# A two-layer gMLP and MLA encoder on one core: the order of its large stages from a list of jobs with due times, with 116 seven-product pairs, activations kept in DRAM and taps by VectorE

## The chip, the cores and the metric

The kernel runs on one core of a Trainium2 chip. The metric is device time in microseconds (us), the median of several runs. Profiles come from one profiled execution. Engines: PE is TensorE, PEld its weight loads, DVE is VectorE, ACT is ScalarE, POOL is GpSimd, SP issues most DMAs.

## What is computed

The input x has 256 tokens of width 2048, in float32. There are two layers. Each has a token mixer and a convolutional feed-forward part; behind each comes `x <- LayerNorm(ALPHA * x + sublayer(x))`.

```python
# layer 0, mixer (gMLP); u and v have 6144 columns, 8 groups, windows of 128 tokens
u, v = split(gelu(x @ w_in), 2);  v = layer_norm(v)
s = einsum('gij,bnjgd->bnigd', w_s * mask, v) + b_s
m = (u * s) @ w_out
# layer 1, mixer (latent attention): 16 heads, ranks 512, chunk-causal softmax, then @ w_out
# both layers, feed-forward (D_FF = 5504)
h = causal_depthwise_conv3(x @ w_up) + conv_b;  a, g = split(h, 2)
f = (silu(g) * a) @ w_down
```

## The kernel before

**Products.** Every float32 operand is split into a high part (float32r) and the low rest; a product is then three matmuls (high × high, high × low, low × high). Activations are kept transposed, as the stationary operand; weights stream as 512 columns. The weights come from DRAM as a list of steps of 128 × 2048 (`Step`, L50), one 1 MiB load each on SP's queue. ScalarE casts a step's high part (`wh`), VectorE subtracts for the low part (`wl`). In the stages v, u and up and in wo and dn a step holds a pair of k-tiles against 1024 output columns, so a plain pair is 2 k-tiles × 2 token blocks × 2 column halves × 3 products, 24 matmuls (`Square.plain`, L469).

**Seven-product pairs.** For some pairs the two k-tiles, two token blocks and two column halves are taken as 2 × 2 blocks and multiplied with seven products instead of eight, Strassen's way (`Square.step`, L477): 21 matmuls. VectorE then also forms sums of weight quarters (four adds of 512 columns, in place in `raw`), ScalarE casts them (`th`), VectorE takes their low part (`tl`); the low part `wl` covers 1536 columns (`Feed._split`, L141). The activations need sums too: `sums_quad` (L432) once for a stage, `sums1` (L438) per pair in wo and dn. Four further PSUM banks (`_p`) collect products and `Square.gather` (L505) adds them together after the last seven-product pair. Which pairs are such is fixed in L236 to L240, where `placed` also says at which of a square's eight steps they stand: v three in five squares of six, u two in six, up two in nine of ten per layer, wo five in each half, dn four in each half.

**Stages.** v and u: six squares of eight steps each (x against 6144 columns each). Behind each v square ScalarE applies gelu and VectorE takes statistics; the six v tiles stay in SBUF until u's gates use them. Behind each u square the `gates` (L862) transpose u, multiply v by the window weights (PE), and form the gated values (VectorE). wo and dn (`Down`, L569 on) run over their k-tiles in two halves of 1024 columns, forward and then backward; `split4` (L397) makes the high and low part of the gate values or activations for each half. up: four steps for the first 512 columns (`boundary`, L653), ten squares of eight steps and two last steps. Behind each up square PE transposes the result into four PSUM banks (`ht`), and `taps` (L928) apply the convolution to four tiles of 128 × 256 at a time: ScalarE makes three scaled copies of each tile, VectorE adds them in two adds of 1020 and 1016 columns per four tiles, ScalarE applies silu, VectorE multiplies. Then come the attention stages (L1049 on), where `scores` (L1252) makes, for each head and token block, five matmuls of 256 columns.

**Order of the work.** Instructions run in program order on each engine. `Feed.next` (L198) is called before each PE step: it splits up to two steps ahead and loads about two more, as far as the 22 slots of 8 KiB a partition (`BIG`) allow. Side work (taps, gates, gathers, statistics) is put at a number of steps from now and at one of three places within a step (`Flow`, L86). All instructions go through one recording line, so rows of the profile show L74; tiles tell them apart.

## Time and profile before

| | us |
|---|---|
| median of 3 runs | 2484.49 (2484.10 to 2484.86) |
| profiled execution | 2485.57 |
| its span, first to last instruction | 2483.8 |
| VectorE, ScalarE busy | 2049.6, 1444.2 |

In the profile a row of a group gives engine, operation, tiles written and read, shape and count, then busy time and the mean duration in ns, then the idle time before it and what ended that. A row of a window gives start and end, its length, then busy time and (xcount) of PE, PEld, DVE, ACT and POOL, the granted PE clock, the DMA share and GB/s. In a timeline the first two numbers are start and duration in us. Durations overlap at their ends: a 512-column matmul shows 0.39 us, and the next one starts 0.23 us after it.

### The profile page before, as it was taken

To read this page: it belongs to the slowest core of one execution; us is meant where nothing else is said; L and a number is where in the kernel's file an instruction comes from. 1 tells how busy PE (TensorE), PEld (TensorE's weight loads), DVE (VectorE), ACT (ScalarE), POOL (GpSimd) and SP (SyncE) were. 2 spreads that over 40 slices of the span, in tenths; PEclk is the share of its full clock that TensorE was granted. 3 is DMA by queue.
4 is the path that set the end of the run, shared out by engine and by line. 5 is a ranking of instruction groups with operands and counts; after the bars stand their busy time and mean duration, and the time that the engine had idled before them with its cause. 6 is when DMAs were issued, how large, how long until landed. Compare 5 with 4: busy or idle time off the path is not lost.

```text
span 2483.8 us, 30045 instructions
## 1 busy us (share of the span) xinstructions
PE 2470.1 (99%) x11666; PEld 2068.6 (83%) x11666; DVE 2049.6 (83%) x2121; ACT 1444.2 (58%) x1673; POOL 1.9 (0%) x11
## 2 busy tenths in 40 slices
PE   9999999999999999999999999999999999999998
PEld 7888888888888888888888888988888888888886
DVE  7899888889797678888899887757768888889796
ACT  6455645555454566666665454555466666667552
POOL 0000000000000000000000000000000000000000
PEclk9999999999999999999999999999999999999999
DMA  7555645555666645555456665435555555556664
GB/s 308 191 193 197 206 167 170 202 171 203 220 214 235 229 166 174 204 186 203 153 198 237 226 237 210 173 136 213 203 174 207 171 187 202 189 196 202 226 205 151
DMA packets 119662, 492.64 MB, mean 198 GB/s; under 512 B 13280, under 2 KB 13664, under 8 KB 104928
## 3 DMA queue, kind: packets, MB, share of 16 engines
q1 hardware_dynamic: 118512, 484.31, 55.6%
q10 hardware_dynamic: 1008, 6.42, 0.6%
q8 instruction: 91, 1.49, 0.2%
q14 instruction: 51, 0.42, 0.0%
HBM read 482.29 MB, written 8.39 MB: 198 GB/s over the span
## 4 chain that ended last, share of the span: by engine, by line
PE 98%; DVE 1%; DMA 0%; ACT 0%; issue 0%; DVEq 0%; ACTq 0%
PE up L74 30%; PE dn L74 16%; PE u L74 9%; PE wo L74 9%; PE v L74 9%; PE up_p L74 4%; PE mo L74 4%; PE upf L74 2%; PE dn_p L74 2%; PE v_p L74 2%; PE ht L74 1%; PE u_p L74 1%; PE wo_p L74 1%; PE mkv L74 1%; PE kn L74 1%; PE qn L74 1%
## 5 line engine op out<-in xcount | busy, mean ns | idle before, releaser
L74 DVE TENSOR_TENSOR wl<-raw,wh 128x2048 fp32r<-128x2048 f32 (+3 forms) x456 | 955.5, 2110 | 216.6 <-ACT wh L74 202.9
L74 ACT CAST wh<-raw 128x2048 fp32r<-128x2048 f32 (+3 forms) x456 | 804.3, 1784 | 187.9 <-DMA raw<-in_ffn_up_dram 54.4
L74 PE MATMUL up<-wh,xhl 128*128 128x512 f32 x2056 | 563.8, 390 | 0.0
L74 PEld LDWEIGHTS up<-wh,xhl 128*128 128x128 f32 x2056 | 384.4, 188 | 78.8
L74 ACT CAST th<-raw 128x1024 fp32r<-128x1024 f32 x178 | 188.5, 1088 | 414.2 <-DVE raw L74 342.1
L74 PE MATMUL up<-wl,xhl 128*128 128x512 f32 x1028 | 319.6, 389 | 0.0
L74 DVE TENSOR_TENSOR raw<-raw 128x512 f32<-128x512 f32 x356 | 246.4, 692 | 12.3
L74 DVE TENSOR_TENSOR tl<-raw,th 128x1024 fp32r<-128x1024 f32 x178 | 214.8, 1222 | 20.7 <-ACT th L74 19.6
L74 PEld LDWEIGHTS up<-wl,xhl 128*128 128x128 f32 x1028 | 192.9, 188 | 40.3
L74 ACT ACTIVATE c<-ht,cst 128x256 f32<-128x256 f32 x320 | 160.0, 591 | 83.2 <-PE ht L74 83.2
L74 PE MATMUL wo<-wh,woa 128*128 128x512 f32 x628 | 173.2, 389 | 0.0
L74 PE MATMUL u<-wh,xhl 128*128 128x512 f32 x600 | 166.1, 391 | 0.0
L74 PE MATMUL dn<-wh,dn0a 128*128 128x512 f32 x576 | 158.3, 389 | 0.0
L74 PE MATMUL dn<-wh,dn1a 128*128 128x512 f32 x576 | 158.0, 389 | 0.0
L74 PE MATMUL v<-wh,xhl 128*128 128x512 f32 x558 | 155.2, 393 | 1.6 <-ACT wh L74 1.6
L74 PEld LDWEIGHTS wo<-wh,woa 128*128 128x128 f32 x628 | 117.7, 188 | 24.3
L74 PEld LDWEIGHTS u<-wh,xhl 128*128 128x128 f32 x600 | 111.9, 188 | 22.7
L74 PEld LDWEIGHTS dn<-wh,dn1a 128*128 128x128 f32 x576 | 108.0, 188 | 22.5
L74 PEld LDWEIGHTS dn<-wh,dn0a 128*128 128x128 f32 x576 | 108.0, 188 | 22.4
L74 PEld LDWEIGHTS v<-wh,xhl 128*128 128x128 f32 x558 | 105.6, 189 | 25.2 <-ACT wh L74 2.8
L74 PE MATMUL wo<-wl,woa 128*128 128x512 f32 x314 | 99.5, 389 | 0.0
L74 PE MATMUL u<-wl,xhl 128*128 128x512 f32 x300 | 93.4, 389 | 0.0
(510 smaller groups left out, 3577.7 us busy)
## 6 DMA issues: line engine op xcount, KB each, us to landing
raw<-in_ffn_up_dram SPq DMA_DIRECT2D x320, 512.0 KB, 4.8
raw<-in_ffn_dn_dram SPq DMA_DIRECT2D x172, 512.0 KB, 4.7
raw<-in_gm_in_dram SPq DMA_DIRECT2D x99, 512.0 KB, 4.9
raw<-in_gm_wout_dram SPq DMA_DIRECT2D x96, 512.0 KB, 4.4
raw<-in_gm_in_dram SPq DMA_DIRECT2D x46, 1024.0 KB, 4.9
raw<-in_ml_out_dram SPq DMA_DIRECT2D x16, 1024.0 KB, 4.8
raw<-in_ml_b_dram SPq DMA_DIRECT2D x14, 1024.0 KB, 4.9
raw<-in_ffn_up_dram SPq DMA_DIRECT2D x12, 1024.0 KB, 6.3
```

The costliest lines, as they stand in the source:

```text
L74: r = f(*args, **kw)
```

## The change

- **Planner.** In v, u, wo, up and dn, `Flow` and the look-ahead of `Feed.next` are replaced by `Plan`: every load, cast, subtraction, sum, gather, output pass, gate and tap is a `Job` with an engine, an estimated cost, predecessors, a due time and the slots (`big`, `bank`, `mid`, `t2`) that it needs and frees. `Plan.run` simulates the engines' clocks and, each time, emits the job whose due time plus three times the idle time that it would cause is least. Transposes (`turn`) are emitted between PE steps when their inputs are reckoned ready, and without fail before a square's first seven-product step. The other stages keep `Flow`.
- **Pairs.** u gets three seven-product pairs per square, four of the ten up squares three and the other six two (the first square included), wo seven and six, dn six and five: 116 for 89.
- **Weight sums.** Of the four 512-column adds two become one of 1024 columns; the gather's last two adds become one.
- **DRAM.** Five of the six v tiles go to DRAM (`park`, on SP's queue) and come back before u's gates. Five of the six wo sources (gate values) and five of the six tiles of feed-forward activations of a layer go to DRAM and come back once for each half. Residual, LayerNorm-row and table loads now keep program order on SP's queue.
- **Taps.** ScalarE makes one scaled copy (tap 2 and bias); the other two taps are multiply-adds by VectorE of 255 and 254 columns that read the transposes' PSUM banks, two for each tile.
- **Scores.** The first token block multiplies only its 128 keys.

The diff, cut to its core:

```diff
-            b21, x, y, b12 = (raw[:, i * 512 : (i + 1) * 512] for i in range(4))
-            b22, b11 = (x, y) if s.by_k else (y, x)
-            first, second = self._pairs(s)
-            ve.tensor_tensor(b11, b11, b12, ALU.subtract)
-            ve.tensor_tensor(b12, b22, b12, ALU.subtract)
-            ac.copy(first(s.th), first(raw))
-            ve.tensor_tensor(b22, b22, b11, ALU.add)
-            ve.tensor_tensor(b21, b21, b22, ALU.subtract)
-            ac.copy(second(s.th), second(raw))
+            q = self._quarters
+            c0, c1, c2, c3 = (raw[:, i * 512 : (i + 1) * 512] for i in range(4))
+            two = raw[:, 512:1536].rearrange("p (a c) -> p a c", a=2)
+            last = c3.rearrange("p (a c) -> p a c", a=1).to_broadcast([P, 2, 512])
+            ve.tensor_tensor(q(raw, 1), two, last, ALU.subtract)
+            ac.copy(q(s.th, 1), q(raw, 1))
+            ve.tensor_tensor(c2, c2, c1, ALU.add)
+            ve.tensor_tensor(c0, c0, c2, ALU.subtract)
+            ac.copy(q(s.th, 0), q(raw, 0))
...
+FIRST_BANKS = (0.0, 0.2, 2.7, 2.9)
+SUM_BANKS = (1.3, 2.0, 2.7, 3.4)
...
+def adds(n, k=1):
+    return k * (0.065 + 0.00106 * n)
+
+
+def copies(n, k=1):
+    return k * (0.07 + 0.00086 * n)
+
+
+def maps(n, k=1):
+    return k * (0.19 + 0.0009 * n)
...
+class Plan:
+    LAG = {"V": 0.16, "A": 0.33, "P": 0.21, "S": 1.9}
+    AHEAD = 60.0
...
+    def _prepare(self, j, load=None):
+        f = self.feed
+        s = f.steps[j]
+        cols = 1536 if s.seven else s.cols
+        after = (load,) if load else ()
+        c = self.chain[j]
+        new = lambda eng, cost, fn, after, kind, **kw: c.append(self.job(eng, cost, fn, after, step=j, kind=kind, **kw)) or c[-1]
+        hi = new("A", copies(cols), lambda: f.cast(j), after, "hi", need={"big": 2})
+        if not s.seven:
+            new("V", adds(cols), lambda: f.low(j), (hi,), "lo", give={"big": 1})
+            return
+        lo = new("V", adds(cols), lambda: f.low(j), (hi,), "lo")
+        one = new("V", adds(1024), lambda: f.sum1(j), (lo,), "t1")
+        th1 = new("A", copies(1024), lambda: f.high(j, 1), (one,), "h1", need={"big": 2})
+        two = new("V", adds(512, 2), lambda: f.sum2(j), (one,), "t2")
+        th2 = new("A", copies(1024), lambda: f.high(j, 0), (two, th1), "h2")
+        l1 = new("V", adds(1024), lambda: f.rest(j, 1), (th1,), "l1")
+        new("V", adds(1024), lambda: f.rest(j, 0), (th2, l1), "l2", give={"big": 1})
+
+    def _more(self):
+        f = self.feed
+        while self.made < min(f.used + 9, len(f.steps), self.last):
+            j = self.made
+            load = self.job("S", 2.9, f._load, self.loads[-1:], step=j, kind="load", need={"big": 1})
+            self.loads.append(load)
+            self.chain[j] = [load]
+            self._prepare(j, load)
+            self.made += 1
+
+    BEFORE = dict(load=12.0, hi=2.9, lo=0.2, t1=4.3, h1=2.7, t2=3.0, h2=1.5, l1=1.4, l2=0.2)
+    SEVEN = dict(hi=7.6, lo=5.6, load=12.0)
...
+            best = {}
+            for j in self.jobs:
+                if any(a.end is None for a in j.after) or not self._fits(j):
+                    continue
+                t = self._start(j)
+                idle = max(t - self.now[j.eng], 0.0)
+                key = (self._due(j) + 3.0 * idle, t)
+                if t > until and must() :
+                    continue
+                if j.eng not in best or key < best[j.eng][0]:
+                    best[j.eng] = key, t, j
...
+    def step(self, fn, after=(), banks=(), force=False):
+
+        f = self.feed
+        i = f.used
+        s = f.steps[i]
+        self.spare = 0
+        self.run(must_true, self.now["P"] - 0.3)
+        if force:
+            self.turnings(True)
+        else:
+            self.turnings()
+        self.spare = len(banks)
+        self._more()
+        must = lambda: (all(j.end is not None for j in self.chain[i]) and len(self.room["bank"]) >= len(banks)
+                        and all(j.end is not None for j in after))
+        self.run(must, self.now["P"])
+        t = max([self.now["P"]] + [j.end for j in self.chain[i]] + [j.end for j in after])
+        for i_, wait in enumerate(banks):
+            t = max(t, self.room["bank"][i_] - wait)
+        del self.room["bank"][: len(banks)]
+        self.spare = 0
+        self.run(must_true, t)
+        f.used += 1
+        fn(s)
+        self.now["P"] = t + s.len
+        del self.chain[i]
+        self.free("big", f.size(i), self.now["P"] + self.LAG["P"])
+        return self.now["P"] + self.LAG["P"]
+
+    def park(self, src, dst, after):
+
+        return self.job("S", 2.9, lambda: self.feed.sq.dma_start(dst, src()), after, due=0.0, give={"big": 1})
+
+    def fetch(self, src, tile, after, due):
+        return self.job("S", 2.9, lambda: self.feed.sq.dma_start(tile, src), after, due=due - 6.0, need={"big": 1})
...
-GROUP_U = [placed((2, 3), (4, 6))] * 6
-GROUP_UP = [placed((), ())] + [placed((2, 3), (4, 6))] * 9
-SEVEN_WO = ((8, 16, 24, 32, 40), (14, 20, 26, 32, 38))
-SEVEN_DN = ((8, 16, 24, 32), (12, 18, 26, 34))
+GROUP_U = [placed((2, 3, 4), (3, 5, 6))] * 6
+GROUP_UP = [placed((2, 3), (5, 6)), placed((2, 3), (4, 6)), placed((2, 3, 4), (4, 5, 6)), placed((2, 3), (4, 6)), placed((2, 3, 4), (4, 5, 6)), placed((2, 3), (4, 6)), placed((2, 3, 4), (4, 5, 6)), placed((2, 3), (4, 6)), placed((2, 3, 4), (4, 5, 6)), placed((2, 3), (4, 6))]
+SEVEN_WO = ((8, 14, 20, 26, 30, 34, 40), (40, 34, 28, 22, 16, 12))
+SEVEN_DN = ((8, 14, 18, 22, 26, 32), (34, 28, 22, 16, 12))
...
-        def gather(self, name):
-
-            e = slot([P, 4, 512], name)
-            u2 = tp.tile([P, 512], F32, tag="t2", name=f"{self.tag}u2", bufs=T2)
+        def gather(self, name, t, due):
+
+            e = self.e = slot([P, 4, 512], name)
             p1, p5, p6, p7 = self.p
-            ac.copy(e[:, 0], p1)
-            ve.tensor_tensor(u2, e[:, 0], p6, ALU.add)
-            ve.tensor_tensor(e[:, 2], u2, p7, ALU.add)
-            ve.tensor_tensor(e[:, 1], u2, p5, ALU.add)
-            ve.tensor_tensor(e[:, 3], e[:, 2], p5, ALU.add)
-            self.e, self.p = e, None
-
-        def out(self, name, func=None):
+
+            def add():
+                ve.tensor_tensor(e[:, 1], e[:, 0], p6, ALU.add)
+                ve.tensor_tensor(e[:, 2], e[:, 1], p7, ALU.add)
+                odd = e.rearrange("p (a b) c -> p a b c", b=2)[:, :, 1]
+                ve.tensor_tensor(odd, e[:, 1:3], p5.rearrange("p (a c) -> p a c", a=1).to_broadcast([P, 2, 512]), ALU.add)
+
+            one = plan.job("A", copies(512), lambda: ac.copy(e[:, 0], p1), ready=t, due=due, need={"big": 1})
+            self.gathered = plan.job("V", adds(512, 2) + adds(1024), add, (one,), due=due + 2, give={"bank": 4})
...
+        if gi < 5:
+            v_out.append(outside(f"vout{gi}"))
+            v_out[gi] = v_out[gi], plan.park(lambda vt=vt: flat(vt), v_out[gi], stat_jobs[-2:])
...
+    def v_back(gi, t):
+
+        after = (root,)
+        if gi < 5:
+            v[gi] = slot([P, 4, 512], f"vb{gi}")
+            after += (plan.fetch(v_out[gi][0], flat(v[gi]), (v_out[gi][1],), t),)
+        scaled[gi] = plan.job("A", maps(1024, 2), lambda: v_scale(gi), after, ready=t - 20, due=t)
...
-            c = slot([P, 2, 4, S], f"c{name}")
-            d = tp.tile([P, 4, S], F32, tag="mid", name=f"d{name}", bufs=MID)
-
-            def scale():
-                for i, (F, src) in enumerate(tiles):
-                    w = C_CONV + (layer * 2 * NF_FF + F) * 4
-                    ac.activation(c[:, 0, i], src, AF.Identity, bias=cst[:, w + 3 : w + 4], scale=cst[:, w + 2 : w + 3])
-                    ac.activation(c[:, 1, i], src, AF.Copy, scale=cst[:, w + 1 : w + 2])
-                    ac.activation(d[:, i], src, AF.Copy, scale=cst[:, w : w + 1])
-
-            y = c[:, 0, 0:n]
+            y = tp.tile([P, 4, S], F32, tag="mid", name=f"y{name}", bufs=MID)
+            w = lambda F, i: cst[:, C_CONV + (layer * 2 * NF_FF + F) * 4 + i :][:, 0:1]
+
+            def scale(i):
+                F, src = tiles[i]
+                ac.activation(y[:, i], src, AF.Identity, bias=w(F, 3), scale=w(F, 2))
+
+            def add(i):
+                F, src = tiles[i]
+                for d in (1, 2):
+                    ve.scalar_tensor_tensor(y[:, i, d:S], src[:, 0 : S - d], w(F, 2 - d), y[:, i, d:S], ALU.mult, ALU.add)
...
+        def tapped(tiles, name, t, bank, after=(), more=0):
+
+            a, m = tiles[0][0], len(tiles) // 2
+            scale, add, silu, gate = taps(tiles, name)
             made = []
-            flow.at(t, "mid", lambda: (made.extend(taps(tiles, f"{layer}_{a}")), made[0]()))
-            for i in range(1, 4):
-                flow.at(t + 1 + i, "mid", lambda i=i: made[i]())
+            for i in range(2 * m):
+                due = plan.wide - 0.4 - 0.7 * (2 * m - 1 - i + 4 * more) if bank else t + 6 + i
+                j = plan.job("A", maps(256), lambda i=i: scale(i), after if i == 0 else (j,), ready=t, due=due - 1.2,
+                             need={} if i else {"mid": 1})
+                made.append(plan.job("V", adds(255, 2), lambda i=i: add(i), (j, *made[-1:]), ready=t, due=due,
+                                     give={} if i < 2 * m - 1 else {"bank": 2} if bank else {"t2": 2}))
+            j = made[-1:]
+            j = (plan.job("A", maps(256 * m), silu, j, due=t + 18, need={"t2": 1}),)
+
+            def gated():
+                gate()
+                for F in range(a, a + m):
+                    gate_jobs[F].end = last.end
+
+            last = plan.job("V", adds(256 * m), gated, (*j, *order[0]), due=t + 20, need={"big": 1} if a % 8 == 0 else {},
+                            give={"t2": 1, "mid": 1})
+            order[0] = (last,)
+            if a % 8 == 6:
+                i = a // 8
+                dn.give(i, lambda: flat8(act[i]), (last,), lambda: slot([P, 4, 2 * S], f"ab{layer}_{i}"),
+                        lambda t: t.rearrange("p a (b c) -> p a b c", b=2))
...
-            o = sc[:, b * S : (b + 1) * S]
-            mm(o, q[:, 0, c], k[:, 0], b == 0, False)
-            mm(o, q[:, 0, c], k[:, 1], False, False)
-            mm(o, q[:, 1, c], k[:, 0], False, False)
-            mm(o, r[:, c], krh, False, False)
-            mm(o, r[:, c], krl, False, b == 1)
+            n = (b + 1) * P
+            o = sc[:, b * S : b * S + n]
+            mm(o, q[:, 0, c], k[:, 0, 0:n], b == 0, False)
+            mm(o, q[:, 0, c], k[:, 1, 0:n], False, False)
+            mm(o, q[:, 1, c], k[:, 0, 0:n], False, False)
+            mm(o, r[:, c], krh[:, 0:n], False, False)
+            mm(o, r[:, c], krl[:, 0:n], False, b == 1)
```

More of the change, by code (lines that the diff above doesn't have):

```diff
@@ new lines, in sum1, with sum2 @@
+    def sum1(self, j):
+        raw = self.raw[j]
+        two = raw[:, 512:1536].rearrange("p (a c) -> p a c", a=2)
+        last = raw[:, 1536:2048].rearrange("p (a c) -> p a c", a=1).to_broadcast([P, 2, 512])
+        self.ve.tensor_tensor(self._quarters(raw, 1), two, last, ALU.subtract)
+    def sum2(self, j):
+        c0, c1, c2 = (self.raw[j][:, i * 512 : (i + 1) * 512] for i in range(3))
+        self.ve.tensor_tensor(c2, c2, c1, ALU.add)
+        self.ve.tensor_tensor(c0, c0, c2, ALU.subtract)
@@ L555, in tock, with square @@
         flow.t += 1
-    def square(tag, order, xs, sums, name, room):
+    def square(tag, order, xs, sums, name, keep):
         sq = Square(tag)
         sevens = [i for i, (_, sv) in enumerate(order) if sv]
+        plan.wide = plan.at(feed.used + (sevens[0] if sevens else 8)) + 1.3
         for i in range(len(order)):
-            s = tick(room(i))
-            sq.step(s, xs, sums, i == len(order) - 1)
+            plan.keep = keep[i]
+            k0 = order[i][0] * 2
+            first = sevens and i == sevens[0]
+            after = (sums[k0][1],) if order[i][1] else ()
+            sq.t = plan.step(lambda s: sq.step(s, xs, {k: r for k, (r, _) in sums.items()}, i == len(order) - 1),
+                             after, FIRST_BANKS if i == 0 else SUM_BANKS if first else (), bool(first))
@@ L564, in square, with __init__ @@
             if sevens and i == sevens[-1]:
-                flow.at(1, "first", lambda: sq.gather(name))
-            tock()
+                sq.gather(name, sq.t, sq.t + 3)
         return sq
     class Down:
-        def __init__(self, n_k, src8, sevens, tag):
-            self.n_k, self.src8, self.sevens, self.tag = n_k, src8, sevens, tag
+        def __init__(self, n_k, gates, sevens, tag):
+            self.n_k, self.gates, self.sevens, self.tag = n_k, gates, sevens, tag
             self.hl, self.sums = {}, {}
-        def need(self, k, half):
+            self.quads = range((n_k + 3) // 4)
+            kept = {k // 4 for k in back_order(n_k, 0)[-KEEP:]}
+            self.left = {}
+            for half in range(2):
+                for i in [q // 2 for q in self.quads if half == 0 or q not in kept] + [k // 8 for k in sevens[half]]:
+                    self.left[half, i] = self.left.get((half, i), 0) + 1
+            self.last = (n_k - 1) // 8
+            self.parked, self.here = {}, {}
@@ new lines, in give, with source @@
+        def give(self, i, tile, after, again, view, stays=None):
+            if stays is not None:
+                self.here[0, i] = self.here[1, i] = stays, ()
+                return
+            dst = outside(f"{self.tag}src{i}")
+            self.parked[i] = dst, plan.park(tile, dst, after), again, view
+        def source(self, i, half, due):
+            if (half, i) not in self.here:
+                dst, job, again, view = self.parked[i]
+                t = again()
+                self.here[half, i] = view(t), (plan.fetch(dst, flat(t), (job,), due),)
+            return self.here[half, i]
@@ L576, in need, with done, f @@
+        def done(self, i, half):
+            def f(t):
+                self.left[half, i] -= 1
+                if self.left[half, i] == 0 and (half == 1 or i != self.last):
+                    plan.free("big", 1, t)
+            return f
+        def need(self, k, half, due):
             q = k // 4
             if q not in self.hl:
-                self.hl[q] = split4(self.src8[k // 8], q, min(4, self.n_k - 4 * q), f"{self.tag}a{half}_{q}")
-        def need_sums(self, k, half):
+                n = min(4, self.n_k - 4 * q)
+                src, after = self.source(k // 8, half, due - 6)
+                self.hl[q] = split4(src, q, n, f"{self.tag}a{half}_{q}",
+                                    {*after, *(self.gates[4 * q + i] for i in range(n))}, due, self.done(q // 2, half))
@@ L609, in run @@
                         if left == 5:
-                            ln.prep()
+                            plan.job("S", 6.0, ln.prep, due=plan.at(feed.used), need={"big": 2})
+                        plan.keep = 3 if 5 < left < 8 else 1
                     if half == 1 and left < LATE:
-                        late.append((s, {k // 4: hl[k // 4]}, left == 0))
-                        tock()
+                        late.append((plan.hold(), {k // 4: hl[k // 4][0]}, left == 0))
                         continue
-                    sq.step(s, hl, sums, left == 0)
+                    first = k in sevens and fresh
@@ L616, in run @@
+                    fresh = fresh and not first
+                    after = [hl[k // 4][1]] + ([sums[k][1]] if k in sevens else [])
+                    t = plan.step(lambda s: sq.step(s, {q: h for q, (h, _) in hl.items()},
+                                                    {q: r for q, (r, _) in sums.items()}, left == 0),
+                                  after, FIRST_BANKS if i == 0 else SUM_BANKS if first else (), first)
                     rest = order[i + 1 :]
```

477 lines of the change are left out of this document (358 added, 119 removed).

## Prediction

> **What bounds the kernel now.** I read the page's shares and its chain of waits first, then who TensorE (PE) waited for, then stretches of steady work in each stage.
>
> ```profile
> span 2483.8 us, 30045 instructions
> PE 2470.1 (99%) x11666; PEld 2068.6 (83%) x11666; DVE 2049.6 (83%) x2121; ACT 1444.2 (58%) x1673; POOL 1.9 (0%) x11
> PE 98%; DVE 1%; DMA 0%; ACT 0%; issue 0%; DVEq 0%; ACTq 0%
> ```
> ```profile
> PE v L74 <- ACT wh L74: 1.6, 1, 1.6
> PE warm L74 <- POOL idle L324: 1.3, 1, 1.3
> ```
>
> The chain that ends last is PE for 98%, and in the whole run PE waited twice, 2.9 us together, at the start. A busy PE alone need not be PE at its rate, so I look at how its matmuls follow one another, and at the other engines by stage (columns: PE, weight load, DVE, ACT, POOL, clock, DMA share, GB/s):
>
> ```profile
> 1305.34 18.36 PE dn L74 x81
> ```
> ```profile
> 0.00:50.00 50.00, 47.01 (x187) 35.85 (x188) 33.42 (x32) 29.23 (x28) 1.90 (x11) 0.97 0.84 332
> 89.29:213.73 124.44, 124.44 (x550) 103.04 (x550) 116.71 (x114) 67.97 (x58) 0.00 (x0) 1.00 0.53 189
> 297.37:487.50 190.13, 190.13 (x937) 160.56 (x937) 158.08 (x176) 102.28 (x109) 0.00 (x0) 1.00 0.51 173
> 557.38:660.00 102.62, 102.62 (x454) 84.94 (x454) 88.49 (x89) 57.16 (x44) 0.00 (x0) 1.00 0.61 220
> 908.95:1216.48 307.53, 307.53 (x1416) 256.29 (x1415) 264.02 (x239) 203.45 (x274) 0.00 (x0) 1.00 0.54 188
> 1260.00:1369.00 109.00, 109.00 (x505) 91.02 (x504) 96.32 (x96) 71.77 (x81) 0.00 (x0) 1.00 0.61 218
> 1369.00:1480.00 111.00, 111.00 (x492) 91.90 (x491) 92.35 (x94) 59.38 (x47) 0.00 (x0) 1.00 0.64 230
> 2473.20:2483.80 10.60, 0.00 (x0) 0.00 (x0) 7.50 (x13) 0.29 (x1) 0.00 (x0) 0.62 0.33 126
> ```
>
> 81 matmuls of 512 columns in 18.36 us are 226.7 ns each, back to back at clock 1.00. PE has no gap in any stage; 10.6 us behind its last matmul are the last LayerNorm and its store, which the change leaves alone. So the time is the count of matmuls times their rate: fewer matmuls shorten the run one for one, unless another engine then fails to feed PE. VectorE (DVE) is the candidate: it is at 94% in v (116.71 of 124.44), 83% in u, 86% in wo's first part, 86% in the up stage and 87% in dn.
>
> **PE's part of the change.** A plain pair of k-tiles takes 24 matmuls (2 k-tiles, 2 token blocks, 2 column halves, 3 products), a seven-product pair 21. Before: v 15, u 12, up 18 per layer, wo 10, dn 8 per layer, 89 in all. After: v 15, u 18, up 24, wo 13, dn 11, 116 in all. 27 × 3 = 81 matmuls go, 18.4 us by the row above. The number of sums that a square gathers costs PE nothing.
>
> The attention scores of the first token block shrink from 256 columns to 128 (16 heads × 5 = 80 matmuls). The trace has the old form, 128-column transposes, and 128-column float32 products:
>
> ```profile
> 1661.49 0.49 PE L74 MATMUL pt<-ident,p 128*128 128x128 f32 x3
> 1661.81 0.82 PE L74 MATMUL o<-pts,vv 128*128 128x256 f32 x4
> ...
> 1663.16 0.52 PE L74 MATMUL sc<-kn,qn 128*128 128x256 f32 x3
> 1663.52 0.40 PE L74 MATMUL sc<-krr,qr 128*128 128x256 f32 x2
> 1663.76 0.52 PE L74 MATMUL sc<-kn,qn 128*128 128x256 f32 x3
> 1664.11 0.40 PE L74 MATMUL sc<-krr,qr 128*128 128x256 f32 x2
> 1664.35 0.63 PE L74 MATMUL mo<-wh,oT 128*128 128x512 f32 x2
> ```
> ```profile
> 356.41 0.39 PE L74 MATMUL s<-wT,v 128*128 128x128 f32 x2
> 356.63 0.27 PE L74 MATMUL uT<-ident,u 128*128 128x128 f32 x1
> ```
>
> Ten score matmuls take 1.19 us, 0.119 each; three transposes of 128 columns take 0.32, 0.107 each, hardly less, as if the weight load of 128 columns set the pace. So I take 80 × 0.012 = 1.0 us off. Ends: by the line through 512 and 256 columns (0.227, 0.119) 128 columns would take 0.065, 4.3 us off; if the short product took float32's path (a pair of s instructions, 0.22), 8.1 us on. The transposes are the nearest row. The Trainium skill (TensorE: Matmul & The Clock Gate, "Back-to-back issue gap") gives about 81 ns for a sustained 128-column stream; by that the estimate would be 3.0 us off in place of 1.0. The transposes at 0.107 speak against it.
>
> Sum for PE: 18.4 + 1.0 = 19.4 us off. The profiled execution took 2485.6 (span 2483.8 and 1.8 around it), 1.1 above the median of the runs; so 2466.2 in its terms, 2465.1 in the median's, if nothing waits.
>
> **What it loads on VectorE.** Rows of seven steady up squares (14 seven-product pairs), one of u and one tile of wo:
>
> ```profile
> L74 DVE TENSOR_TENSOR wl<-raw,wh 128x2048 fp32r<-128x2048 f32 x43 | 97.7, 2287 | 1.2 <-ACT wh L74 1.2
> L74 DVE TENSOR_TENSOR raw<-raw 128x512 f32<-128x512 f32 x56 | 38.8, 692 | 2.0
> L74 DVE TENSOR_TENSOR tl<-raw,th 128x1024 fp32r<-128x1024 f32 x28 | 33.5, 1222 | 7.2 <-ACT th L74 7.2
> L74 DVE TENSOR_TENSOR wl<-raw,wh 128x1536 fp32r<-128x1536 f32 x14 | 24.6, 1755 | 32.4 <-ACT wh L74 32.4
> L74 DVE TENSOR_TENSOR c<-c,d 128x1016 f32<-128x1016 f32 x14 | 17.0, 1218 | 0.5
> L74 DVE TENSOR_TENSOR c<-c 128x1020 f32<-128x1020 f32 x14 | 17.0, 1215 | 0.0
> ```
> ```profile
> L74 DVE SCALAR_TENSOR_TENSOR sg<-s,cst,sb 128x256 f32<-128x256 f32 x32 | 13.9, 478 | 17.5 <-PE s L74 17.5
> ```
> ```profile
> L74 DVE TENSOR_TENSOR wos_14t<-v,wos_14t x1: 293/293/293, 736.0 to 736.0; 128x128 f32<-128x128 f32 x1
> L74 DVE TENSOR_TENSOR wos<-wos_14t,wos x1: 686/686/686, 740.7 to 740.7; 128x512 fp32r<-128x512 f32 x1
> ```
>
> - A pair made seven: low part 1.76, sums 1.22 (two quarters at once, priced as the 1024-wide row) + 2 × 0.69, tl 2 × 1.22, less the plain low part 2.29: +4.5 us. A pair that was seven saves 0.17 (one 1024-wide sum for two of 512), a gather 0.15 likewise.
> - Taps: the two adds of four tiles go, 34.0/7 = 4.9 us per square; 16 multiply-adds of 255 columns out of PSUM come, nearest row sg, 13.9/32 = 0.43 apart (0.48 alone): 7.0 (7.7). +2.1 us (+2.8). ScalarE loses two of three tap passes, so it is no bound.
> - A wo or dn pair also needs its activation sums: 4 × 0.29 + 0.69 = 1.85.
>
> u: 158.08/4 = 39.5 per square of 47.5; +4.5 − 0.5 gives 43.5 in 46.9 (93%). wo: 86% to about 92%. dn: 188.7 of 220, +3 × (4.5 + 1.85) − 1.7 gives 206 of 218 (95%). up: 264.02/7 = 37.7 of 43.9; with two sevens 39.3, with three (four of ten squares) 43.8 against PE's 43.25: over by 0.6. The kinds alternate, so two squares want 83.1 of 87.2 (95%). Below 100% everywhere once neighbours share; v ran at 94% with no wait of PE. What hides the new work is thus VectorE's idle time, plus the split steps ahead of PE. If that cover fails in the eight overfull squares alone, 8 × 0.6 = 5 us come on; I take 2 us, nearer to v's none.
>
> **DMA and its queue.** Gate values and activations leave in 20 transfers of 1 MiB (5 v, 5 wo sources, 5 per dn) and come back in 35: 58 MB on top of
>
> ```profile
> DMA packets 119662, 492.64 MB, mean 198 GB/s; under 512 B 13280, under 2 KB 13664, under 8 KB 104928
> ...
> raw<-in_ffn_up_dram SPq DMA_DIRECT2D x320, 512.0 KB, 4.8
> ...
> parked<-res ACTq DMA_DIRECT2D x6, 1024.0 KB, 6.1
> res<-parked SPq DMA_DIRECT2D x6, 1024.0 KB, 7.4
> ```
>
> wo gets most: ten fetches in some 225 us add 47 GB/s to 220; the first 50 us carried 332. So bandwidth is no bound. The new thing is order: SP's queue is serial, and a store that waits for VectorE's or ScalarE's last gate now holds every weight load queued behind it. A load that slips by one PE step (24 × 0.227 = 5.4 us) still lands (4.8) within that step, and the freed SBUF slots let loads run further ahead; zero, and 20 × 0.6 = 12 us if each store held a load two steps and the landing 0.6 us were all uncovered. I keep zero as value. The residual, LayerNorm-row and table loads now keep their place in the same queue; all are due some steps ahead of use: zero.
>
> **Forecast.** 2465.1 + 2 = 2467 us. Unknown sizes alone reach from 2461 (scores −4.3 in place of −1.0, no waits) to 2476 (scores +8.1).
>
> **Rivals.**
> (B) VectorE's idle share cannot go under the 6.2% of v. Then a pair of up squares takes 83.1/0.938 = 88.6 in place of 87.2, 1.4 × 8 = 11 us; dn 206/0.938 = 219.6 in place of 218, 1.6 × 2 = 3; u at 93% just fits. 2465.1 + 14 = 2479, and less if it binds in part. For: v is the fullest stage shown. Against: v's idle time there was no need, PE never waited.
> (C) Half of today's idle time stays because it is latency between engines:
>
> ```profile
> DVE wl L74 <- ACT wh L74: 33.6, 9, 4.9
> ```
>
> In those seven squares VectorE idled 43.5 us, mostly on that line. With half, 3.1 per square: 83.1 + 6.2 − 87.2 = 2.1 × 8 = 17 us in up, and u 43.5 + 4.0 − 46.9 = 0.6 × 6 = 4: 2486, no change. Against: the list puts other work into such waits. The Trainium skill (Perfetto Trace Analysis, "Identifying the Most-Contended Engine") judges TensorE by its weight loads, 83% here, level with VectorE, and so would take an edit that loads VectorE for a poor trade; PE's two short waits show that as yet VectorE limits nothing.
> (D) Slower. The planner prices a tap multiply-add at 0.335 us (its formula for 255 columns) where the sg row has 0.43: it believes the 16 taps of a square done 1.6 us before they are. Until then they hold the four PSUM banks that the square's first seven-product step needs, and PE's next matmul stands behind that wait. If VectorE has no slack left there, 1.6 × 20 squares = 32 us: 2497. It decides from 19.4/20 = 1.0 us per square on. Against: the taps are due before that step, four plain steps (21.8 us) lie ahead of it, and VectorE has in that time 7.0 us of taps and six 512-wide adds and gates (4.1 us at 0.69).
> That the change did not remove what it says would show as 11666 matmuls again; the lists of pairs leave no room for it.
>
> **How the numbers follow.** Forecast with its sizes (2461 to 2471): 0.60. B, whole or in part (2471 to 2479.5): 0.15. C (2479.5 to 2489.5): 0.09. D and other stalls beyond: 0.16. Runs of this kernel lie 0.8 us apart; 0.2%, 5 us, is about what a measurement can tell. Faster 0.75, same 0.09, slower 0.16. Range 2461 to 2485: it leaves out D above, about half of C, and little below.
>
> **What would show it.** Right: 11585 matmuls; PE idle under 20 us in all; VectorE near 95% in up and dn; ScalarE's busy time down; scores' first five matmuls about 0.107 apart; DMA near 550 MB. Wrong: PE waiting on wl or tl in up squares with three sevens (B, C), or on an ht bank that VectorE's taps still read at the first seven-product step (D), or weight casts waiting on raw loads behind a store.

## The result, and the profile after

The changed kernel takes 2467.11 us (median of 4 runs, 2466.72 to 2467.49), the kernel before 2484.40 beside it: 17.3 us less, a ratio of 0.993 with a 95% interval of 0.9917 to 0.9942. The profiled execution took 2466.72.

The page of the changed kernel, its shares, chain, DMA total and PE's waits:

```profile
span 2464.9 us, 30098 instructions
PE 2449.7 (99%) x11585; PEld 2053.0 (83%) x11585; DVE 2218.2 (90%) x2459; ACT 1375.1 (56%) x1388; POOL 1.9 (0%) x11
...
DMA packets 127583, 550.33 MB, mean 223 GB/s; under 512 B 14160, under 2 KB 14544, under 8 KB 105808
...
PE 99%; DVE 1%; DMA 0%; issue 0%; ACT 0%; DVEq 0%
```
```profile
PE v L75 <- ACT wh L75: 1.6, 1, 1.6
PE warm L75 <- POOL idle L646: 1.3, 1, 1.3
PE lnt L75 <- DVE res L75: 1.0, 1, 1.0
```

81 matmuls are gone, VectorE carries 168.6 us more, ScalarE 69 less, and PE's waits come to 3.9 us in all, one wait more than before. The stretches that answer to those of before (u, the beginning of wo, seven up squares, two of these squares, dn in two parts, the end; the same columns):

```profile
295.33:482.75 187.42, 187.42 (x926) 158.42 (x925) 173.33 (x185) 108.97 (x118) 0.00 (x0) 1.00 0.65 225
551.94:650.00 98.06, 98.06 (x435) 81.21 (x434) 95.09 (x100) 60.18 (x49) 0.00 (x0) 1.00 0.68 246
899.88:1204.69 304.81, 304.81 (x1403) 254.22 (x1403) 288.93 (x320) 169.15 (x168) 0.00 (x0) 1.00 0.57 203
943.13:1030.31 87.18, 87.18 (x402) 72.71 (x402) 82.31 (x92) 48.39 (x49) 0.00 (x0) 1.00 0.58 204
1247.00:1356.00 109.00, 109.00 (x506) 91.08 (x505) 105.92 (x123) 66.39 (x66) 0.00 (x0) 1.00 0.72 264
1356.00:1465.00 109.00, 109.00 (x483) 90.34 (x482) 99.26 (x100) 58.18 (x47) 0.00 (x0) 1.00 0.72 261
2454.30:2464.90 10.60, 0.00 (x0) 0.00 (x0) 7.52 (x14) 0.29 (x1) 0.00 (x0) 0.58 0.35 135
```

PE's busy time equals each stretch's length (except at the end), at clock 1.00, as before; VectorE is at 92% in u, 97% in wo's beginning, 94% in two up squares and 94% in dn (205.2 of 218.0).

Where the 18.8 us between the two spans come from, in us, by the first matmul of each stage (before and after; mo is the last stage of attention, and its row and that of the second dn end at the start of their last matmul):

| stage | before | after | shorter by |
|---|---|---|---|
| all ahead of u | 0 to 261.16 | 0 to 259.81 | 1.35 |
| u | to 540.99 | to 535.56 | 4.08 |
| wo | to 801.78 | to 794.05 | 2.30 |
| up, layer 0 | to 1279.32 | to 1267.52 | 4.07 |
| dn, layer 0, and what follows | to 1533.45 | to 1520.78 | 0.87 |
| attention, to mo's last matmul | to 1766.35 | to 1753.13 | 0.55 |
| up, layer 1 | to 2244.45 | to 2227.15 | 4.08 |
| dn, layer 1 | to 2472.73 | to 2453.39 | 2.04 |
| behind the last matmul | to 2483.76 | to 2464.93 | -0.51 |

The 1.35 us ahead of u can't be put down to the change, as the first 20 us show; three kernels in turn, before, after, and first_square_two (an experiment below, the changed kernel up to u):

```profile
0.00:20.00 20.00, 17.01 (x58) 11.72 (x59) 11.14 (x12) 12.42 (x15) 1.38 (x10) 0.91 0.92 354
```
```profile
0.00:20.00 20.00, 16.98 (x64) 11.61 (x65) 10.79 (x12) 12.08 (x14) 1.38 (x10) 1.00 0.89 345
```
```profile
0.00:20.00 20.00, 17.31 (x56) 12.07 (x57) 10.86 (x12) 12.18 (x15) 1.38 (x10) 1.00 0.90 353
```

PE does 58, 64 and 56 matmuls in these 20 us; the difference of 8 between the last two kernels, whose code is the same there, is 1.8 us at 0.227, and u begins at 259.8 and 261.6. In the profiles of the kernels below whose code ahead of u is the changed kernel's, u begins between 259.3 and 261.9. So medians that lie under 2 us apart are read by stage below.

From u on the spans differ by 17.5 us.

### The profile page after: what moved, and what is told of

The parts are those of the page before. It is cut to its first block, busy times and chain, and to the rows that moved or that the text cites. A ratio compares the mean times of both kernels' runs of the same rounds, so it can differ in the third digit from the quotient of the medians.

```text
span 2464.9 us, 30098 instructions
## 1 busy us (share of the span) xinstructions
PE 2449.7 (99%) x11585; PEld 2053.0 (83%) x11585; DVE 2218.2 (90%) x2459; ACT 1375.1 (56%) x1388; POOL 1.9 (0%) x11
## 2 busy tenths in 40 slices
DMA packets 127583, 550.33 MB, mean 223 GB/s; under 512 B 14160, under 2 KB 14544, under 8 KB 105808
## 4 chain that ended last, share of the span: by engine, by line
PE 99%; DVE 1%; DMA 0%; issue 0%; ACT 0%; DVEq 0%
PE up L75 29%; PE dn L75 15%; PE wo L75 9%; PE v L75 9%; PE u L75 8%; PE up_p L75 5%; PE mo L75 4%; PE dn_p L75 2%; PE u_p L75 2%; PE upf L75 2%; PE v_p L75 2%; PE wo_p L75 1%; PE ht L75 1%; PE mkv L75 1%; PE kn L75 1%; PE qn L75 1%
## 5 line engine op out<-in xcount | busy, mean ns | idle before, releaser
L75 PE MATMUL up<-wh,xhl 128*128 128x512 f32 x1888 | 522.1, 391 | 0.0
L75 ACT CAST th<-raw 128x1024 fp32r<-128x1024 f32 x232 | 244.1, 1053 | 378.8 <-DVE raw L75 376.9
L75 PEld LDWEIGHTS up<-wh,xhl 128*128 128x128 f32 x1888 | 353.2, 188 | 72.0
L75 DVE TENSOR_TENSOR raw<-raw 128x1024 f32<-128x1024 f32 x348 | 302.0, 868 | 9.0
L75 PE MATMUL up<-wl,xhl 128*128 128x512 f32 x944 | 295.0, 390 | 0.0
L75 DVE TENSOR_TENSOR tl<-raw,th 128x1024 fp32r<-128x1024 f32 x232 | 281.3, 1220 | 0.2 <-ACT th L75 0.2
L75 DVE SCALAR_TENSOR_TENSOR y<-ht,cst,y 128x255 f32<-128x255 f32 x320 | 147.5, 479 | 13.0 <-ACT y L75 7.2
L75 PE MATMUL u<-wh,xhl 128*128 128x512 f32 x516 | 145.2, 391 | 0.0
L75 ACT ACTIVATE y<-ht,cst 128x256 f32<-128x256 f32 x160 | 78.0, 574 | 94.7 <-PE ht L75 94.7
L75 PE MATMUL up_p<-th,xs 128*128 128x512 f32 x288 | 96.6, 389 | 0.0
```

Source lines behind the costliest of these rows:

```text
L75: r = f(*args, **kw)
```

## The experiments

All are compared with the kernel before on their chip (2484.7 to 2485.3 us); the changed kernel's 2467.11 is the mark.

**Pairs and order, each without the other.** The changed kernel with the old lists of pairs:

```diff
-GROUP_U = [placed((2, 3, 4), (3, 5, 6))] * 6
-SEVEN_WO = ((8, 14, 20, 26, 30, 34, 40), (40, 34, 28, 22, 16, 12))
-SEVEN_DN = ((8, 14, 18, 22, 26, 32), (34, 28, 22, 16, 12))
...
+GROUP_U = [placed((2, 3), (4, 6))] * 6
+GROUP_UP = [placed((), ())] + [placed((2, 3), (4, 6))] * 9
+SEVEN_WO = ((8, 16, 24, 32, 40), (14, 20, 26, 32, 38))
+SEVEN_DN = ((8, 16, 24, 32), (12, 18, 26, 34))
```

> The changed kernel with the pair lists of before (89 seven-product pairs, not 116); planner, DRAM trips, VectorE taps and short scores stay. Theory (the time is PE's matmuls, and the 27 pairs are the whole gain): 81 matmuls of 226.7 ns come back, 18.4 us, so 2467.1 + 18.4 = 2485.5 us, VectorE's busy time some 115 us lower, no new wait of PE. Rival (the order, the DRAM trips or the taps bring a good part of the gain by themselves): clearly below 2480 us.

2484.17 us, ratio 0.9998 (0.9989 to 1.0008), with 11666 matmuls. VectorE is busy for 2083.2 us, 135 less than in the changed kernel, where 115 were expected. Planner, weight sums, DRAM, taps and scores together change nothing that shows in the time (by stages the shorter scores save 0.6 us); the 17 us come only when the pairs are there. The opposite, the same edit reversed in the kernel before:

> The kernel before with the pair lists of the change (116 pairs); fixed look-ahead, v and activations in SBUF, taps by ScalarE, long scores. Rival (VectorE stays below 100% of each stage, u at 44.0 of 46.9 us, so the old order feeds the pairs as well): 2484.4 - 18.4 = 2466 us. Theory (share below 100% is not enough; the fixed look-ahead of two steps and the 22 slots, of which u's stage holds 12 for x, its sums and v, leave VectorE idle when it could work ahead): PE waits appear, above all in u and in up squares with three such pairs, and the time is above 2480 us, perhaps 2500.

2548.74 us, ratio 1.0258 (1.0243 to 1.0274). Its page and PE's waits:

```profile
PE 2478.7 (97%) x11585; PEld 2050.6 (81%) x11585; DVE 2200.1 (86%) x2356; ACT 1488.4 (58%) x1732; POOL 1.9 (0%) x11
```
```profile
PE up L74 <- DVE wl L74: 17.6, 18, 3.2
PE up_p L74 <- DVE tl L74: 12.1, 15, 1.0
PE u L74 <- DVE wl L74: 9.1, 11, 0.8
PE dn L74 <- DVE wl L74: 7.7, 6, 1.3
```

VectorE has 18 us less to do than in the changed kernel, and yet PE waits on its low parts in u, up and dn. The first up square of a layer takes 49.9 and 49.3 us where the changed kernel takes 42.65; of the others, those with two such pairs take 43.94 us (the last 44.3) and those with three 47.6 to 49.6, where the changed kernel takes 43.94 and 43.25. Under the old order the idle time of a light square doesn't help the next one. So neither half is worth anything alone: 0.5 us for all that isn't pairs, 64 us lost for the pairs, 17 gained with both. Which parts of the other half the pairs need was looked at for the v tiles in DRAM and for the taps alone; the planner without the DRAM trips of wo and dn wasn't run.

**Activations in DRAM.** The v tiles stay in SBUF as before (their stores and loads go):

```diff
-        if gi < 5:
+        if False:
```

> The changed kernel, but the five v tiles stay in SBUF and are not sent to DRAM and back (10 transfers fewer, five slots fewer in u). Theory A (the freed slots carry the look-ahead that three pairs in u need): waits of PE in u, several us, above 2472 us. Theory B (slots are not what limits u; VectorE's share, 93%, is the same): 2467 us, no change.

2480.0 us, ratio 0.9981 (0.9971 to 0.999). PE's waits, 25 us at u's beginning, and VectorE's longest wait from 262 to 305 us:

```profile
PE u_p L75 <- DVE tl L75: 6.4, 3, 2.4
PE u_p L75 <- ACT th L75: 1.9, 1, 1.9
```
```profile
275.00:300.00 25.00, 21.05 (x87) 16.77 (x86) 18.08 (x15) 13.33 (x11) 0.00 (x0) 0.90 0.61 208
```
```profile
DVE wl L75 <- ACT wh L75: 6.8, 3, 5.0
```

From its first matmul to wo's, u takes 288.1 us (259.2 to 547.3) in place of 275.8. VectorE is busy for only 18.08 of 25 us in which PE waits for what it makes, because it waits itself for ScalarE's casts. These wait, in the same stretch, 10.2 us for matmuls of u (7.8 ahead of `wh`, 2.4 ahead of `th`) and 7.8 us for one weight load. A cast that waits for PE waits for a slot that PE still reads, so what is lacking is slots to work ahead in, which the edit takes away. The freed slots are worth 12 us in u; no wait of PE in the changed kernel shows a price for the added DMA.

**One step further ahead** at the end of dn, aimed at the new wait on `lnt`:

```diff
-                        plan.last = end_at + 2
+                        plan.last = end_at + 3
```

> The changed kernel, where the last half of wo and dn may load three steps of the next stage and not two. In the changed kernel PE waits 1.0 us for a LayerNorm row at the end of the first dn, because VectorE splits two late-loaded steps ahead of the residual sum. Theory: the third step is loaded and split earlier, the wait goes, 1.0 us less (2466.1). Rival: the extra load takes a slot that the last dn steps need, no gain or a wait elsewhere.

2467.15 us (ratio 0.9928, 0.9914 to 0.9943), and the wait is there with 1.0 us as before: a miss. The timeline of the changed kernel at that place shows why:

```profile
1483.28 4.48 DVE L75 TENSOR_TENSOR wl<-raw,wh 128x2048 fp32r<-128x2048 f32 x2
...
1487.68 0.68 DVE L75 TENSOR_TENSOR res<-res,dn 128x512 f32<-128x512 f32 x1
...
1491.09 0.66 PE L75 MATMUL lnt<-ident,res 128*128 128x128 f32 x4 [1.02 <-DVE res L75]
```

VectorE makes two low parts of the next stage (4.48 us) ahead of the residual sum that the LayerNorm and then PE wait for. By the semaphores in the trace the matmul that completes this sum's input ends at 1486.0, so the sum comes 1.7 us late, held by the second of the two. That is a matter of the order of jobs at that place, which the limit on look-ahead doesn't reach; another order there wasn't tried.

**Who does the taps.** ScalarE makes three scaled copies again and VectorE two adds for four tiles, as before the change; their jobs' costs, slots and banks follow, and the rest is as changed:

```diff
-                for d in (1, 2):
-                    ve.scalar_tensor_tensor(y[:, i, d:S], src[:, 0 : S - d], w(F, 2 - d), y[:, i, d:S], ALU.mult, ALU.add)
+                ac.activation(c[:, 1, i], src, AF.Copy, scale=w(F, 1))
+                ac.activation(dd[:, i], src, AF.Copy, scale=w(F, 0))
...
+                ve.tensor_tensor(y[:, :, 1:S], y[:, :, 1:S], c[:, 1, 0:n, 0 : S - 1], ALU.add)
+                ve.tensor_tensor(y[:, :, 2:S], y[:, :, 2:S], dd[:, 0:n, 0 : S - 2], ALU.add)
```

> The changed kernel with the taps as before: ScalarE makes three copies of each tile, VectorE two adds per four tiles, one slot of 22 more for each four tiles; the pairs and the planner stay. VectorE's work falls by some 2.8 us per up square, ScalarE's rises by some 8. Theory (VectorE is below its limit either way and ScalarE has room): no change, 2466 to 2468 us. Rival (the taps had to move for the pairs to fit: the slot or ScalarE's longer hold of the banks shows): waits of PE in up, above 2472 us.

2468.64 us (ratio 0.9934, 0.9919 to 0.9949); up squares at 43.94 and 43.25 as in the changed kernel. From u's first matmul to dn's last the two profiles agree within 0.1 us (2193.6); what this one is longer by lies ahead of u (it begins at 261.9) and, 0.7 us, behind the last matmul. The move of the taps brought nothing and cost nothing.

**How full VectorE can be.** First with more taps: the first multiply-add is done twice for every other tile (taps_four_extra) or for every tile (taps_eight_extra), which changes the convolution's values; the planner doesn't count it.

```diff
-                for d in (1, 2):
+                for d in (1, 1, 2) if i % 2 == 0 else (1, 2):
```

> The changed kernel, where VectorE does the first tap's multiply-add twice for two of each four tiles (the output is then not the reference's): 4 more per square at 0.48 us, 1.9 us, of which the planner knows nothing. Two up squares then want 82.3 + 3.8 = 86.1 of PE's 87.2 us, 98.8%. Theory (VectorE's limit is its sum over neighbouring squares): no change, 2467 to 2469 us. Rival D of the prediction (taps that end later than planned hold the PSUM banks of the first seven-product step, one for one): up to 20 x 1.9 us, 2505 us, with waits at that step.

2476.9 us, ratio 0.9967 (0.9955 to 0.9978), between the two theories. Two up squares:

```profile
950.84:1038.79 87.95, 87.82 (x402) 72.51 (x401) 86.62 (x100) 48.44 (x49) 0.00 (x0) 1.00 0.57 203
```

They take 87.95 us for 86.6 of VectorE's work, 98.5%, where PE alone needs 87.19. Of the time that comes on, 2.9 and 2.5 us lie in the two up stages and 2.0 and 2.6 in the dn behind them, where PE waits on `wl` (2.6 us).

```diff
-                for d in (1, 2):
+                for d in (1, 1, 2):
```

> The changed kernel, where VectorE does the first tap's multiply-add twice for every tile (output not the reference's): 8 more per square, 3.8 us, unknown to the planner. Two up squares want 90.0 of 87.2 us, 103%. Theory: VectorE now limits the up stage; 2.8 us for each of ten pairs of squares, 28 us, less what the steps split ahead cover at the start, so about 2485 to 2495 us. Rival (VectorE's work is hidden in any case): 2467 us. Rival D: 20 x 3.8 us, 2543 us.

2518.81 us, ratio 1.0135 (1.0118 to 1.0151), more than the first theory's 2485 to 2495 and less than rival D's 2543. Two squares and the waits:

```profile
954.89:1046.80 91.91, 88.70 (x402) 72.28 (x401) 90.36 (x108) 48.17 (x49) 0.00 (x0) 1.00 0.55 194
```
```profile
PE up_p L75 <- DVE tl L75: 16.9, 24, 1.2
PE up L75 <- DVE wl L75: 10.0, 18, 1.1
```

91.9 us pass for 90.4 of work, 98.3%. PE waits for weights that VectorE prepares too late, not at the transposes' banks, where rival D had put it.

Then with more pairs: three in each of the ten up squares, 12 more pairs (here and below the changed kernel's list of ten is the line left out):

```diff
...
+GROUP_UP = [placed((2, 3, 4), (4, 5, 6))] * 10
```

> The changed kernel with three seven-product pairs in all ten up squares of both layers: 12 more pairs, 36 matmuls or 8.2 us less for PE. VectorE's work by the changed kernel's trace: two squares (one of two, one of three pairs) 82.3 us, so a square of three is 43.4 us against PE's 43.25, 100.4%. Theory (VectorE limits only from 100% on, and what it lacks is covered by steps split ahead): 2459 to 2463 us. Rival (an idle share of 6% is unavoidable for VectorE): squares of 46.3 us, 20 x 3 us longer, about 2520 us.

2486.9 us, ratio 1.0009 (1.0 to 1.0018): a miss, some 24 us above the range. PE's longest wait, and the first square of each layer:

```profile
PE up_p L75 <- DVE tl L75: 9.9, 4, 4.4
```
```profile
850.00:875.00 25.00, 20.07 (x81) 15.77 (x80) 24.83 (x22) 12.23 (x9) 0.00 (x0) 0.93 0.46 155
1825.00:1850.00 25.00, 22.72 (x98) 18.84 (x99) 24.24 (x27) 12.09 (x15) 0.00 (x0) 0.86 0.37 128
```

VectorE is full in both windows and PE starved, 81 and 98 matmuls where the changed kernel does 120 in each. No lead has been built up there. PE waits 4.9 us in each of the two squares, and the granted clock is 0.50 for 3.4 and 6.8 us behind the waits (means of 0.93 and 0.86 over 25 us). The first squares take 49.2 and 50.3 us. The next four take 43.25 to 43.30, no loss; from then on each takes 43.8 to 43.9. To tell the first square from the steady load, it is given two pairs and the other nine three (the new lists are written in short here and below; the edits spell out their ten entries):

```diff
...
+GROUP_UP = [placed((2, 3), (5, 6))] + [placed((2, 3, 4), (4, 5, 6))] * 9
```

> Edit to the changed kernel: the first up square of each layer has two seven-product pairs, the other nine have three (three_in_every_up_square had three in all ten). Theory A: there the loss lay in the first square of each layer, which has no lead over PE (about 7.3 us per layer, with half the granted clock behind it), and in a drift of about 0.5 us per square once the lead is spent; with a light first square the 7.3 us go twice and the drift stays: 2486.9 - 14.6 = 2472 us, and 2468 to 2476 with it. PE waits on up_p in the first square gone. Theory B: nine squares at three in a row overload VectorE wherever they stand (43.8 us of work, with a ceiling of 98% that is 44.7 us per square, 0.8 of them lost to PE's 43.94 on each): 2483 us or more.

2473.56 us, ratio 0.9956 (0.9942 to 0.9969), as the first theory had it. Three stretches of two squares each, from the second square's second step on:

```profile
869.29:955.80 86.51, 86.51 (x400) 72.11 (x398) 85.32 (x96) 49.17 (x49) 0.00 (x0) 1.00 0.59 207
955.80:1043.04 87.24, 87.08 (x400) 71.87 (x398) 86.23 (x97) 50.35 (x50) 0.00 (x0) 1.00 0.58 205
1043.04:1130.72 87.68, 87.29 (x399) 71.80 (x398) 86.70 (x97) 50.34 (x50) 0.00 (x0) 1.00 0.58 204
```

PE needs 86.51. While VectorE can live on its lead (98.6% here) it gets it; after three squares the lead is spent, and 87.7 us pass for 86.7 of work, 98.9%. Each layer's up stage is then as long as in the changed kernel (473.8 and 473.5 us from its first matmul to dn's, for 473.5 and 473.4), with 15 matmuls less in it: what the five added pairs save is given back in full. dn lost 1.5 us in each layer, with waits on `wl`, and 2.4 more lie behind the last matmul, where the planner put the last residual sum behind the other block's LayerNorm.

**Using what is left.** Six of ten squares at three (in order 2, 2, 3, 3, 3, 2, 3, 3, 3, 2), four more pairs in all:

```diff
...
+GROUP_UP = [placed((2, 3), (5, 6))] + ([placed((2, 3), (4, 6))] + [placed((2, 3, 4), (4, 5, 6))] * 3) * 2 + [placed((2, 3), (4, 6))]
```

> Edit to the changed kernel: six of the ten up squares of a layer take three seven-product pairs (order 2,2,3,3,3,2,3,3,3,2) where four did. Four more pairs, 12 fewer matmuls, 2.7 us at 0.227. Theory A (VectorE can be used to 98% over neighbouring squares): three threes and a two want 3 x 43.5 + 39.0 = 169.5 us of VectorE in 173.7 of PE, 97.6%, just under; all 2.7 us show: 2464.4 us. Theory B (what limits is the longest run of threes: three in a row are over by 0.3 to 0.6 us each, and the lead does not carry that far): 1 to 2 us per run of three come on, four runs: 2468 to 2472 us.

2466.13 us, ratio 0.9925 (0.9913 to 0.9938). Four squares (2, 3, 3, 3) late in the stage, in layer 0 and in layer 1:

```profile
1040.59:1215.81 175.22, 174.81 (x801) 144.40 (x800) 169.44 (x188) 99.12 (x98) 0.00 (x0) 1.00 0.58 207
2000.40:2174.10 173.70, 173.70 (x801) 144.78 (x800) 169.62 (x188) 99.12 (x98) 0.00 (x0) 1.00 0.59 209
```

The same code and the same work of VectorE: at 97.7% once with no loss, once with 1.5 us lost. Layer 1 keeps its 1.4 us, layer 0 doesn't; the time lies between the two theories, nearer the first, and what the first had as "just under" is the edge itself.

Why the two layers differ is seen where VectorE stands idle. In both windows the only waits that its profile lists are for the copy (`h`) with which ScalarE begins a square's gather, layer 0 first; below them is layer 0's longest:

```profile
DVE h L75 <- ACT h L75: 3.8, 2, 3.1
```
```profile
DVE h L75 <- ACT h L75: 2.1, 1, 2.1
```
```profile
1074.69 1.91 ACT L75 CAST wh<-raw 128x2048 fp32r<-128x2048 f32 x1 [4.89 <-DMA raw<-in_ffn_up_dram]
1076.50 0.58 ACT L75 COPY h<-up_p 128x512 f32<-128x512 f32 x1
...
1077.11 2.67 DVE L75 TENSOR_TENSOR h<-h,up_p 128x512 f32<-128x512 f32 x3 [3.07 <-ACT h L75]
```

ScalarE has a cast ahead of that copy, and the cast waits for its weight load: 4.89 us in layer 0, 3.94 at the same place in layer 1. VectorE stands behind both. In the next kernel the code of up is the same; there VectorE waits 3.0 us for `h` in layer 0 and 2.2 in layer 1, and the four squares lose 0.8 us and nothing. So 2.1 and 2.2 us of such idle time cost nothing, 3.0 cost 0.8 and 3.8 cost 1.5. No edit tested this, and why the load comes later in layer 0 isn't known.

And with a sixth pair in dn's second half as well:

```diff
-SEVEN_DN = ((8, 14, 18, 22, 26, 32), (34, 28, 22, 16, 12))
+SEVEN_DN = ((8, 14, 18, 22, 26, 32), (34, 30, 26, 22, 16, 12))
```

> As six_of_ten_threes, and dn's second half takes six seven-product pairs for five, in both layers: 6 matmuls less, 1.4 us. Theory A (ceiling 98%): dn's second half, now 99.26 of 109.0 us (91%), gets 6.35 more, 97%: 1.4 us below six_of_ten_threes, 2463.0 us. Theory B (dn's pairs also need activation sums and its second half must prepare the next stage's first steps): the gain is lost in the boundary behind dn; equal to six_of_ten_threes or up to 2 us above it.

2464.40 us (2463.2 to 2464.83), ratio 0.9917 (0.9904 to 0.9931), the fastest kernel here, 2.7 us below the changed one by the medians; the intervals of the two ratios overlap. By stages, dn is 0.7 us shorter in each layer (252.6 for 253.3; 238.7 for 239.4 from up's last matmul on), up by 0.6 and 1.1: in dn it is as the first theory had it. Another 0.6 us is gained behind the last matmul.

**The scores** at full width again for the first token block:

```diff
-            n = (b + 1) * P
+            n = S
```

> Edit to the changed kernel: the attention scores of the first token block go back to 256 columns. By the traces of the two kernels ten score matmuls took 1.19 us before and 1.15 after, and the whole stage about 0.6 us less for 16 heads: 0.6 us up, 2467.7 us, and the first five matmuls of a head 0.119 apart again. The prediction's size gives 1.0 us up; a sustained 128-column rate of 81 ns would give 3.0 us up, 2470.

2469.21 us (2467.34 to 2469.39), ratio 0.9935 (0.992 to 0.995). Of the 2.1 us, 1.2 lie ahead of u (261.0 for 259.8) and 0.5 in wo, neither of which has scores; from the first score to mo's last matmul 134.1 us pass, for 133.5: 0.6 us. One head in the changed kernel, and in this one:

```profile
1640.45 0.45 PE L75 MATMUL sc<-kn,qn 128*128 128x128 f32 x3
...
1640.96 0.57 PE L75 MATMUL sc<-kn,qn 128*128 128x256 f32 x3
...
1641.60 0.63 PE L75 MATMUL mo<-wh,oT 128*128 128x512 f32 x2
```
```profile
1642.35 0.52 PE L75 MATMUL sc<-kn,qn 128*128 128x256 f32 x3
...
1642.94 0.52 PE L75 MATMUL sc<-kn,qn 128*128 128x256 f32 x3
...
1643.54 0.63 PE L75 MATMUL mo<-wh,oT 128*128 128x512 f32 x2
```

Five short ones take 0.51 us (0.102 each) for 0.59, but the five long ones behind them 0.64 for 0.60: 1.15 for 1.19 in all.

## Why the prediction was right, step by step

- **PE bounds the kernel, and 81 matmuls are 18.4 us.** Right. u, wo, up and dn should have given 4.1, 2.0, 4.1 and 2.0 us per layer by their pairs; u gave 4.1, wo 2.3, up 4.1 in both layers, and dn 2.0 in layer 1 and 0.9 in layer 0, the latter with the 1.0 us wait on `lnt` in it. That the other edits bring nothing without the pairs is shown by old_pairs_new_order.
- **Scores, 1.0 us.** The length of the matmul hardly matters, as said, and the size was too high: 0.55 to 0.6 us. (That the weight load sets the pace was the prediction's guess; no run here tests it.) The short ones are 0.102 apart, even less than the transposes' 0.107, but the following five lose a part of it again, which no row of before could show. The Trainium skill's 81 ns (TensorE: Matmul & The Clock Gate, "Back-to-back issue gap") isn't reached here, and the 3.0 us worked out from it aren't there in either pair of kernels (before and after, scores_full_width and after).
- **VectorE's load.** 82.3 us for two up squares (83.1 was worked out), 205.2 in dn (206), 92% in u (93%). A square with three pairs wants 43.4 us, half of the 86.7 in first_square_two, not 43.8; it is over PE's 43.25 by 0.1, not 0.6. wo's first 98 us are at 97% where 92% was said, wo as a whole is at 93%, 240.5 of 258.5 us:

```profile
535.60:794.10 258.50, 258.50 (x1171) 214.91 (x1169) 240.53 (x252) 144.00 (x120) 0.00 (x0) 1.00 0.68 247
```

  The taps took the upper of the two prices:

```profile
L75 DVE SCALAR_TENSOR_TENSOR y<-ht,cst,y 128x254 f32<-128x254 f32 x48 | 23.1, 482 | 1.7
L75 DVE SCALAR_TENSOR_TENSOR y<-ht,cst,y 128x255 f32<-128x255 f32 x48 | 22.9, 476 | 0.8 <-ACT y L75 0.8
```

  96 in six squares take 46.0 us, 7.7 per square, not 7.0.
- **Waits, 2 us.** 1.0 us on `lnt` and 0.5 behind the last matmul, which the prediction took to be left alone; none in the squares with three pairs, where the 2 us had been put. The place was wrong, the size near: 18.4 + 0.6 - 1.0 - 0.5 = 17.5 us, and 17.5 lie between the spans from u on. That 2467 us was met to 0.1 is luck: the scores gave 0.4 less than said, the waits cost 0.5 less and stood at another place, and where u begins shifts by up to 2.6 us between profiles.
- **DMA and its queue, nothing.** Right: 550.33 MB, and no wait of PE on a load. SP's queue did stand behind gates (87.2 us in eight waits on `act`, 32.6 in five on `v`), and none of it reached PE. It isn't free for all that: ScalarE's casts wait 211 us for weight loads in the changed kernel, 124 before, and at the edge such a wait counts (six_of_ten_threes).
- **Rival B** (6.2% of VectorE's time can't be used) fell: wo's first 98 us ran at 97% with no wait. Where VectorE holds up PE, 1 to 2% of its time stays unused: it reaches 98.9% with nine squares of three pairs, 98.3 and 98.5% with added taps, and 97.7% is on the edge.
- **Rival C** (the waits between ScalarE and VectorE stay) fell for this order, and is what happens under the old one. VectorE's wait of a low part for the cast, over the whole run, in the kernel before, in new_pairs_old_order, in old_pairs_new_order and in the changed kernel:

```profile
DVE wl L74 <- ACT wh L74: 202.9, 104, 10.4
```
```profile
DVE wl L74 <- ACT wh L74: 150.4, 88, 5.0
```
```profile
DVE wl L75 <- ACT wh L75: 142.3, 95, 7.0
```
```profile
DVE wl L75 <- ACT wh L75: 42.1, 46, 5.6
```

  With the pairs alone the waits fall by a quarter, with all but the pairs by 30%, with both by four fifths: the list of jobs fills them with other squares' work, when there is such work. C had priced half of the idle time left in the up squares. In seven of them 15.9 us are left of 43.5, none of it on the cast (9.8 us are on the copy `h` of the gather), and PE waits for none of it. The Trainium skill's way of finding the contended engine judges TensorE by its weight loads or by the arithmetic done, and the others by their busy share (Perfetto Trace Analysis, "Identifying the Most-Contended Engine"). By weight loads it would name VectorE after the change, 90% beside 83%; PE's 3.9 us of waits say that PE still bounds it.
- **Rival D** (the planner's price for the taps is too low, and the banks are held): the price is too low as said, 0.335 against 0.48, and costs nothing at 94%. With four extra taps per square, 1.9 us, 9.8 us come on in all, about half of them in the up stages, 0.3 per square; with eight 51.7, of which 2.0 per square in up. D's point, 1.0 us lost per square, lies between the two, 2 to 4 us of unseen work per square away from the changed kernel. But the wait is on weights, because VectorE as a whole is full, not on the banks.

What stays open: why a weight load comes later in layer 0 than in layer 1, how much of v's 12 us is the number of slots and how much the time at which they come free, and what the DRAM trips of wo and dn are worth.

## What to carry to other kernels

Work that goes from a bounding engine to a second one was worth its whole time here as long as the second stayed below its limit over a few neighbouring stretches of work, and nothing from there on: in up 94% lost nothing, 97.7% was the edge, and what five more pairs saved was given back. At the edge it isn't the share alone that decides but how long the second engine stands waiting in its program order. Whether the second engine can be filled that far was a matter of order and of slots to work ahead in, so judge such an edit together with the order it needs: here each alone was worth nothing or cost 64 us. Look at the first stretch of a stage by itself, where no lead exists yet.

## What was not expected of the hardware

- Behind waits of 4.4 us PE's granted clock was 0.50 for 3.4 us in one layer and 6.8 in the other (three_in_every_up_square), with matmuls 0.427 us apart for 0.227. So a stall cost more than its length: PE waited 4.9 us in each of these squares, and they took 49.2 and 50.3 us where PE needs 42.0 (42.65 with two pairs, less the 0.68 of a third).
- VectorE ran at 98 to 99% of the time over whole squares, with PE losing 0.6 us per square; the 94% of stage v was no limit of its own.
- Five 256-column matmuls take 0.64 us behind five short ones and 0.60 behind long ones.
- The first 20 us hold 55 to 66 matmuls in kernels with the same code there, and u begins up to 2.6 us earlier or later for it.
